# Hybrid encoder layer on one core: small operations of the attention stage issued some shares later, and the embedding's last product taken bank by bank

## The chip, the cores and the metric

One core of a Trainium2 chip runs the whole layer. The metric is the device time of one execution in microseconds; for the kernel before, the median of three runs is 1230.82 us.

## The reference

One post-norm encoder layer in float32 on 1024 tokens of width 1024:

```
u   = x @ W_in                                     # q,k,v,gate of 8 retention heads; q,k,v of 8/2 attention heads
R   = bidirectional chunkwise retention (chunks of 128), group norm, times silu(gate)
A   = windowed grouped attention (+-128 tokens), ALiBi, sink logit
h   = LN1(alpha*x + concat(R, A) @ W_out)
f   = (silu(h@W_gate) * (h@W_up)) @ W_down  +  sigmoid(h @ W_pg) * (p @ W_pe)
out = LN2(alpha*h + f)
```

The second term of f is the per-token embedding gate: W_pg is 1024 x 1024, p is 1024 x 256.

## The kernel before

Products of float32 matrices are made of three matmuls: each operand is split into a rounded part hi (an ACT copy) and a rest lo (a DVE subtraction), and `mm3` (L78) or `mm3c` (L847) multiplies hi*hi, hi*lo and lo*hi. `split` (L72) issues the two operations.

The program has these stages, in order of time:

- the first projections (to about 60 us);
- attention and retention, in "runs" (60 to 375 us): first Attention 0, then Retention 0, then three pairs of Retention i and Attention i;
- the output projection with LN1 (375 to 475 us);
- the embedding gate (to about 590 us), which is a one-level Strassen product: seven products `product(p, ...)` of 48 matmuls each into sets of four PSUM banks, then half tiles `embed(t, h, ...)`;
- gate/up of the feed-forward part and the down projection (to the end), Strassen again, in an order written out by hand.

In the attention stage only TensorE's order is written out (`manual_schedule` for PE); the other engines' order is made by the framework's planner, from its own estimate of times. The same planner orders all engines, PE too, in the embedding gate. `behind(ins)` (L83) adds no wait: it tells the planner to place an instruction after the latest `mm3`. A function `run(steps, total)` goes through a list in which each F (None) is a *share*: `total` projection steps (one `mm3` each) are spread evenly over the shares, and after each share one entry of the list `side` is executed. `side` carries the presplits: `presplit_small` splits p and W_pe, `presplit_gate` makes the seven Strassen operands of W_pg for four contraction tiles k, each with 7 splits and 4 DVE sums, and stores them to DRAM. Its entries are one load, one empty share and seven splits per k. Raw weights pass through `rawt`, two buffers of the tag raw.

Names in the attention stage: `Attention.scores(n)` multiplies (L499, L500), applies bias and maximum on DVE (L501), exponentiates on ACT (L505), takes the reciprocal of the sum (L507) and scales (L509); `turn(n)` transposes the scaled block (L517); `values(n)` multiplies with v (L529). `Retention.keys(q)` transposes keys (L378) and decays them (kdec, L381), `kv(q)` multiplies (L392) and masks (L396), `scores(hh)` makes pt (L420) and qq (L423), `out` accumulates, `norm(hh)` normalises: sums, squares, the power -0.5 on POOL (L463) and the product with it (L464). `turn(hh)` transposes and evicts to y (L471). The decay tables qd and dt are made in `Retention.__init__` (L362 to L370), with POOL's mask product and sum.

In the embedding gate, `stream` loads split operands through eight weight buffers (w and u). `product` has two forms: bank outermost (each bank finished before the next) and, with `outer=True`, contraction outermost. `embed(t, h, x, ...)` multiplies p's tile with W_pe (6 matmuls), takes sigmoid(x) on ACT (L905), multiplies (L906) and adds into the accumulator (L908), and stores the whole accumulator tile to the DRAM buffer zd (L910) after its second half. For the first four half tiles p comes through tag p, two buffers of 256 KB (L899); for the last twelve through tag ln, two buffers of 512 KB that hold two token tiles each (L889). The last product (p=3) carries eight half tiles, two behind each bank; four more follow it. `s1`, an operand of eight of them, lies in the two raw buffers. The first gate/up weights are loaded by `Pair.load` (L981) into raw and ln buffers, called in the preparation of the first units.

Of the kernel before, what the change touches and what calls it, by code (L numbers as in the profile page):

```python
# [16 lines left out]
P = 128  # L17
# [12 lines left out]
NSC = 4  # L30

# [9 lines left out]
def layer(tc, xT, xn, w_first, w_mt, w_rv, w_out, w_pg, w_pe, pT, w_gu, w_dn,  # L41
# [310 lines left out]

    class Retention:


        def __init__(self, i, y):
            self.i, self.y = i, y
            self.rk, self.rq, _ = pairs[i]
            self.A = [bt([P, NT - 1, P], f"kv{d}") for d in range(2)]
            self.kdec, self.pt, self.qq, self.ym = {}, {}, {}, {}  # L360
            self.qd = bt([P, 2, P], "qd")
            for d, c in ((0, C_QF), (1, C_QB)):  # L362
                act.activation(self.qd[:, d, :], cst[:, c:c + P], AF.Exp, scale=lg[:, 16 + 4 * d + i:17 + 4 * d + i])
            self.dt = bt([P, 2, P], "dt")
            for h in range(2):
                e = bt([P, 2, P], "sq", 1)
                act.activation(e[:, 0, :], cst[:, C_DP:C_DP + P], AF.Exp, scale=lg[:, 2 * i + h:2 * i + h + 1])
                act.activation(e[:, 1, :], cst[:, C_DN:C_DN + P], AF.Exp, scale=lg[:, 8 + 2 * i + h:9 + 2 * i + h])
                pool.tensor_tensor(e, e, masks, ALU.mult)
                pool.tensor_tensor(self.dt[:, h, :], e[:, 0, :], e[:, 1, :], ALU.add)  # L370
# [80 lines left out]
        def norm(self, hh):  # L451
            o = self.o
            og = o.rearrange("p n (h e) -> p (n h) e", h=2)
            sm = bt([P, 3, 8], "sm", 2)
            dve.tensor_reduce(sm[:, 0, :], og, AX.X, ALU.add, negate=True)
            ym = self.ym[hh] = bt([P, 8, 64], "ym", 2)
            dve.scalar_tensor_tensor(ym, sm[:, 0, :].unsqueeze(2).to_broadcast([P, 8, 64]), 1.0 / 64, og,
                                     ALU.mult, ALU.add)
            sq = bt([P, 8, 64], "sq", 1)
            act.activation(sq, ym, AF.Square)  # L460
            dve.tensor_reduce(sm[:, 1, :], sq, AX.X, ALU.add)
            dve.tensor_scalar(sm[:, 1, :], sm[:, 1, :], 1.0 / 64, EPS, ALU.mult, ALU.add)  # L462
            pool.tensor_tensor(sm[:, 2, :], sm[:, 1, :], cst[:, C_MH:C_MH + 1].to_broadcast([P, 8]), ALU.pow)  # L463
            dve.tensor_tensor(ym, ym, sm[:, 2, :].unsqueeze(2).to_broadcast([P, 8, 64]), ALU.mult)  # L464
# [12 lines left out]
    class Attention:  # L477
# [6 lines left out]
        def scores(self, n):  # L484
# [22 lines left out]
            dve.reciprocal(st_[:, 3, j, :], st_[:, 2, j, :])  # L507
            for g in range(2):
                act.activation(sc[g][:, :nk], sc[g][:, :nk], AF.Copy, scale=st_[:, 3, j, g:g + 1])  # L509
# [38 lines left out]
    def presplit_small():  # L548

        o = a_tile([P, 2, HF], "pro", "A0", F32R)  # L550
        hold = {}

        def load(n):
            r = hold[n] = rawt(2 * HF)
            if n < 2:
                for j in range(4):
                    sp.dma_start(r[:, j * 2 * P:(j + 1) * 2 * P], pT[4 * n + j])
# [6 lines left out]
        return [f for n in range(4) for f in (lambda n=n: load(n), None, lambda n=n: step(n, 0), None, None,  # L564
                                              lambda n=n: step(n, 1))]

    def presplit_gate():

        raw = [a_tile([P, 2, HF], "pre", "A1") for _ in range(2)]
# [3 lines left out]
        def load(k):  # L573
            for j in range(2):
                sp.dma_start(raw[j], w_pg[j, k])

        def steps(k):

# [10 lines left out]
            return [lambda: load(k), None, s(1, a11), s(4, a22), s(2, a12), s(5, a22, (a22, a21, a22, ALU.add)),  # L589
# [3 lines left out]
        return [f for k in range(4) for f in steps(k)]  # L593
# [35 lines left out]
    def run(steps, total):  # L629

        shares = steps.count(None)
        done = n = 0
        for f in steps:
            if f is None:
                n += 1
                take(total * n // shares - done)
                done = total * n // shares
                if side:
                    (side.pop(0) or (lambda: None))()
            else:  # L640
                f[0](*f[1:])

    F = None
    with tc.manual_schedule(engines={mybir.EngineType.PE}):
# [7 lines left out]
             F, trn(6), F, trn(7), F, val(6), val(7), F], 64)  # L652
        assert not side
        side.extend(presplit_gate())
        r = Retention(0, ytile(0))
# [4 lines left out]
             Y(0, 0), F, Y(0, 1), N(0), F, Q(1), F, F, Y(1, 0), F, Y(1, 1), N(1), F, F], 48)  # L660
        for i in range(1, NPAIR):
            if i == 2:
# [3 lines left out]
            a = Attention(i, ytile(2 * i + 1))  # L666
            run([K(0), Q(0), F, X0, F, C(0), F, X1, K(1), F, C(1), sco(0), F,
                K(2), F, C(2), sco(1), F, K(3), F, trn(0), sco(2), F, C(3), (r.scan,), F, trn(1), F,
                sco(3), F, val(0), val(1), F, trn(2), Y(0, 0), F, sco(4), F, Y(0, 1), N(0), trn(3), F, sco(5), F,
                val(2), val(3), Q(1), F, trn(4), F, F, sco(6), F, trn(5), F, Y(1, 0), F, sco(7), F, val(4), val(5), F,  # L670
                Y(1, 1), N(1), trn(6), F, trn(7), F, F, val(6), val(7)], 48)
# [212 lines left out]
    ptile = {}  # L884

    def load_p(j):

        ptile[j] = ct([P, 2, HF], "ln", 2, F32R)
        sp.dma_start(ptile[j].bitcast(F32), ptd[j])  # L889

    def embed(t, h, x, wpe, tag):

        if ptile:
            if t % 2 == 0:
                load_p(t // 2)
            pt = ptile[t // 2][:, :, (t % 2) * 2 * P:(t % 2 + 1) * 2 * P]
        else:
            pt = ct([P, 2, 2 * P], "p", 2, F32R)
            sp.dma_start(pt.bitcast(F32), ptd[t // 2][:, :, (t % 2) * 2 * P:(t % 2 + 1) * 2 * P])  # L899
# [9 lines left out]
        if h == (0 if t >= 4 else 1):  # L909
            sp.dma_start(zd[t], accs[t])  # L910

    def pair_of(f, g):
        def both():
            f()
            g()
        return both
# [15 lines left out]
    for k in range(4):  # L932
        embed(k, 0, X[k], wpe, "to"[k % 2])
    Z = four("b")
    product(5, Z, True, TT[1], steps[4:6])
# [8 lines left out]
    product(4, Y, False, TT[4])  # L944
    add4(s1, s1, Y)
    wpe = [stream(ped[1, q]) for q in range(2)]
    ptile[-1] = None
    both_ = [pair_of(lambda t=t, x=x: embed(t, 1, x[t % 4], wpe, "mm"), lambda t=t, x=x: embed(t + 1, 1, x[t % 4 + 1], wpe, "s"))
             for t, x in ((0, s1), (4, c22), (2, s1), (6, c22))]
    product(3, Z, False, HB[1, 1], both_)  # L950
    wpe0 = [stream(ped[0, q]) for q in range(2)]
# [546 lines left out]
```

## Time and profile before

| | us |
|---|---|
| median of three runs | 1230.82 (1227.77 to 1234.38) |
| the profiled execution | 1232.8 |
| its span, first to last instruction | 1231.0 |
| TensorE busy | 1202.4 (98%) |
| VectorE (DVE) busy | 732.0 (59%) |
| ScalarE (ACT) busy | 510.1 (41%) |
| GpSimd (POOL) busy | 366.7 (30%) |
| mean granted TensorE clock | 0.992 |

A row of the timeline has the start, the time, the engine, the line, the operation and its tiles; brackets give how long the engine sat idle before it and what ended that. SPq is the queue of SyncE, which issues the loads and stores in order. A row of waits has the waiting engine and line, what ended the wait, the total, the number and the longest. DVE and ACT run their instructions in order, so an instruction that waits holds up those behind it.

### The profile page before, as it was taken

How to read it: one execution, taken by the hardware profiler on the slowest of the kernel's cores; microseconds unless marked ns; L12 is line 12 of the kernel's file. 1: busy time of each engine (PE TensorE's matmuls, PEld its weight loads, DVE VectorE, ACT ScalarE, POOL GpSimd, SP SyncE). 2: the span in 40 equal slices, each digit the busy share in tenths (PEclk: the TensorE clock that was granted, in tenths of full speed). 3: DMA queues.
4: the chain of work that ended last, by engine and by line, in shares of the span. 5: the costliest groups of instructions: out<-in, count | busy, mean ns of one | idle time of the engine just before them, and what ended most of it. 6: DMA issues, size and time to landing. Idle time of an engine off the chain costs nothing.

```text
span 1231.0 us, 16420 instructions
## 1 busy us (share of the span) xinstructions
PE 1202.4 (98%) x5939; PEld 995.7 (81%) x5939; DVE 732.0 (59%) x1262; ACT 510.1 (41%) x960; POOL 366.7 (30%) x342
## 2 busy tenths in 40 slices
PE   9999989999999999999799999999999999999996
PEld 7878878888888888787688888888888888888885
DVE  4542688765646387946655544555445555875667
ACT  4565246655775114302333332332323334652463
POOL 2000021201110020000566656466565523034232
PEclk9999999999999999999899999999999999999999
DMA  6243446410103315467431133322233149999977
GB/s 244 69 139 130 150 164 224 170 35 18 35 18 122 101 52 208 143 247 239 155 128 70 69 118 128 129 78 77 103 129 129 69 145 279 383 277 212 258 181 205
DMA packets 67568, 179.48 MB, mean 146 GB/s; under 512 B 7968, under 2 KB 10144, under 8 KB 67488
## 3 DMA queue, kind: packets, MB, share of 16 engines
q1 hardware_dynamic: 58848, 161.66, 37.1%
q0 software_dynamic: 8640, 16.78, 7.7%
q8 instruction: 47, 0.77, 0.2%
q14 instruction: 33, 0.27, 0.1%
HBM read 125.72 MB, written 47.45 MB: 141 GB/s over the span
## 4 chain that ended last, share of the span: by engine, by line
PE 88%; DVE 4%; DMA 3%; ACT 2%; issue 1%; POOL 1%; SPq 0%; DVEq 0%; ACTq 0%; POOLq 0%
PE bmm L79 6%; PE bmm L80 5%; PE bmm L81 5%; PE bmm L849 5%; PE bmm L850 5%; PE bmm L851 5%; PE bs L849 5%; PE bs L851 5%; PE bs L850 5%; PE bo L851 4%; PE bo L850 4%; PE bo L849 4%; PE bt L849 4%; PE bt L851 4%; PE bt L850 4%; PE bo L529 1%
## 5 line engine op out<-in xcount | busy, mean ns | idle before, releaser
L79 PE MATMUL bmm<-H,w 128*128 128x512 f32 x240 | 100.6, 419 | 0.6 <-ACT H L73 0.6
L81 PE MATMUL bmm<-H,w 128*128 128x512 f32 x240 | 94.6, 394 | 0.0
L80 PE MATMUL bmm<-H,w 128*128 128x512 f32 x240 | 94.4, 393 | 0.0
L989 POOL TENSOR_TENSOR H<-ln 128x512 f32<-128x512 f32 x22 | 29.4, 1335 | 193.6 <-DMA ln<-in_w_gu 193.6
L1019 POOL TENSOR_TENSOR ev<-ev 128x512 f32<-128x512 f32 x33 | 55.7, 1687 | 92.4 <-DVE ev L1034 40.9
L74 DVE TENSOR_TENSOR w<-raw,w 128x512 fp32r<-128x512 f32 x64 | 50.5, 798 | 53.4 <-ACT w L73 53.2
L496 POOL COPY sc<-skb 128x1 f32<-128x1 f32 x64 | 16.7, 269 | 209.2 <-PE bt L517 187.0
L74 DVE TENSOR_TENSOR w<-H,w 128x512 fp32r<-128x512 f32 x44 | 39.6, 900 | 62.7 <-ACT w L73 62.7
L1017 ACT ACTIVATE ev<-ev 128x512 f32<-128x512 f32 x33 | 20.9, 633 | 104.8 <-DVE ev L1034 104.8
L1023 POOL TENSOR_TENSOR ev<-ev,ev 128x512 f32<-128x512 f32 x44 | 62.0, 1420 | 2.6
L74 DVE TENSOR_TENSOR u<-H,u 128x512 fp32r<-128x512 f32 x47 | 36.5, 777 | 38.7 <-ACT u L73 38.4
L501 DVE CUSTOM_DVE_ANT_0 sc<-cst,bs,skb 128x384 f32<-128x384 f32 (+1 forms) x64 | 35.3, 576 | 31.0 <-PE bs L500 30.9
L81 PEld LDWEIGHTS bmm<-H,w 128*128 128x128 f32 x240 | 45.3, 189 | 10.2
L79 PEld LDWEIGHTS bmm<-H,w 128*128 128x128 f32 x240 | 45.4, 189 | 9.8 <-ACT H L73 1.5
L73 ACT ACTIVATE w<-raw 128x512 fp32r<-128x512 f32 x64 | 39.3, 623 | 31.4 <-PE bmm L81 13.0
L80 PEld LDWEIGHTS bmm<-H,w 128*128 128x128 f32 x240 | 45.6, 190 | 6.3
L505 ACT ACTIVATE sc<-sc,st 128x385 f32<-128x385 f32 (+1 forms) x64 | 37.1, 582 | 27.2 <-DVE st L503 27.1
L73 ACT ACTIVATE u<-H 128x512 fp32r<-128x512 f32 x47 | 29.6, 631 | 39.7 <-PE bs L851 11.1
L721 POOL TENSOR_TENSOR stt<-stt,cst 128x1 f32<-128x1 f32 x8 | 11.6, 1454 | 97.9 <-DVE stt L720 97.9
L74 DVE TENSOR_TENSOR u<-raw,u 128x512 fp32r<-128x512 f32 x26 | 31.9, 1226 | 10.4 <-ACT u L73 10.4
L463 POOL TENSOR_TENSOR sm<-sm,cst 128x8 f32<-128x8 f32 x8 | 14.6, 1830 | 77.4 <-DVE sm L462 77.4
L993 POOL TENSOR_TENSOR H<-raw,H 128x512 f32<-128x512 f32 x22 | 37.4, 1698 | 0.0
(819 smaller groups left out, 3764.6 us busy)
## 6 DMA issues: line engine op xcount, KB each, us to landing
ad<-ev SPq DMA_DIRECT2D x33, 512.0 KB, 2.6
pgd<-pro SPq DMA_DIRECT2D x28, 512.0 KB, 2.9
raw<-in_w_gu SPq DMA_DIRECT2D x22, 512.0 KB, 4.3
ln<-in_w_gu SPq DMA_DIRECT2D x22, 512.0 KB, 3.5
raw<-ad SPq DMA_DIRECT2D x40, 256.0 KB, 5.6
ln<-ad SPq DMA_DIRECT2D x37, 256.0 KB, 6.5
H<-in_w_dn SPq DMA_DIRECT2D x33, 256.0 KB, 7.1
raw<-in_w_mt SPq DMA_DIRECT2D x14, 512.0 KB, 3.9
```

What stands on the lines that cost most here:

```text
L73: act.activation(hi, raw, AF.Copy)
L74: dve.tensor_tensor(lo, raw, hi.bitcast(F32), ALU.subtract)
L79: pe.matmul(o, lh, rh, start=start, stop=False)
L80: pe.matmul(o, lh, rl, start=False, stop=False)
L81: recent[0] = pe.matmul(o, ll, rh, start=False, stop=stop).ins.name
L505: act.activation(sc[g][:, :nk + 1], sc[g][:, :nk + 1], AF.Exp, bias=st_[:, 1, j, g:g + 1], accum_out=st_[:, 2, j, g:g + 1])
L849: pe.matmul(o, lh, rh, start=start, stop=False, skip_group_check=True)
L850: pe.matmul(o, lh, rl, start=False, stop=False, skip_group_check=True)
L851: pe.matmul(o, ll, rh, start=False, stop=stop, skip_group_check=True)
L993: pool.tensor_tensor(s[3], a(0, 1), s[0], ALU.subtract)
L1019: pool.tensor_tensor(c[:, 1, :], c[:, 0, :], c[:, 1, :], ALU.mult)
L1023: pool.tensor_tensor(self.ev[dst][:, 0, :], left, right, op)
```

## The change

Five things are changed together.

1. **Later issue in the attention stage.** `run` keeps a list `later`: an entry is executed a given number of shares after it was put there. The reciprocal and the two scalings of a softmax block go two shares later (LAG), the last product of a retention norm too. The decay tables of pair i+1 are made at the end of pair i (`decay_q`, `decay_k`), those of pair 0 at the end of Attention 0. All these are placed `behind` the latest `mm3`.
2. **presplit_small** begins four shares later and has one empty share less per load.
3. **presplit_gate**: tiles k=0 and k=1 are loaded ahead of Retention 0 (k=1 into two buffers of its own, tag A0) and split in its 14 shares without a pause; k=2 is loaded at share 8 and split from pair 1's share 2 on, every second share; k=3 follows.
4. **Embedding, products 5 and 4** have the contraction outermost.
5. **Embedding, the last product**: after each of its four banks, `last_tiles(k)` adds what completes a block and issues two, four, three and three half tiles. All p tiles come through tag p (two buffers of 256 KB, `load_p(t)`), every half tile stores its half of zd, W_pe's two halves are loaded together, and after the first and second bank the first gate/up loads are issued.

```diff
+    def decay_q(i):
+        qd = bt([P, 2, P], "qd")
+        decays[i] = qd, bt([P, 2, P], "dt")
+        for d, c in ((0, C_QF), (1, C_QB)):
+            behind(act.activation(qd[:, d, :], cst[:, c:c + P], AF.Exp, scale=...))
+    def decay_k(i, h):
+        e = bt([P, 2, P], "sq", 1)
+        behind(act.activation(e[:, 0, :], ..., AF.Exp, ...))
+        behind(act.activation(e[:, 1, :], ..., AF.Exp, ...))
+        pool.tensor_tensor(e, e, masks, ALU.mult)
+        pool.tensor_tensor(decays[i][1][:, h, :], e[:, 0, :], e[:, 1, :], ALU.add)
 ...
-            dve.tensor_tensor(ym, ym, sm[:, 2, :]..., ALU.mult)
+            later.append([2, lambda: behind(dve.tensor_tensor(ym, ym, sm[:, 2, :]..., ALU.mult))])
 ...
-            dve.reciprocal(st_[:, 3, j, :], st_[:, 2, j, :])
-            for g in range(2):
-                act.activation(sc[g][:, :nk], sc[g][:, :nk], AF.Copy, scale=st_[:, 3, j, g:g + 1])
+            def scaled():
+                behind(dve.reciprocal(st_[:, 3, j, :], st_[:, 2, j, :]))
+                for g in range(2):
+                    behind(act.activation(sc[g][:, :nk], sc[g][:, :nk], AF.Copy, scale=st_[:, 3, j, g:g + 1]))
+            later.append([LAG, scaled])
 ...
-        return [f for n in range(4) for f in (load(n), None, step(n, 0), None, None, step(n, 1))]
+        return [None] * 4 + [f for n in range(4) for f in (load(n), None, step(n, 0), None, step(n, 1))]
 ...
-        raw = [a_tile([P, 2, HF], "pre", "A1") for _ in range(2)]
+        first, other = ([a_tile([P, 2, HF], "pre", t) for _ in range(2)] for t in ("A1", "A0"))
 ...
-            return [lambda: load(k), None, s(1, a11), s(4, a22), s(2, a12), s(5, ...), s(7, ...), s(6, ...), s(3, ...)]
-        return [f for k in range(4) for f in steps(k)]
+            return [s(1, a11), s(4, a22), s(2, a12), s(5, ...), s(7, ...), s(6, ...), s(3, ...)]
+        load(0)
+        load(1)
+        k0, k1, k2, k3 = map(steps, range(4))
+        k1[0] = pair_of(k1[0], lambda: load(2))
+        return k0 + k1 + [None] + gap(k2, range(6)) + [lambda: load(3), None, None] + gap(k3, (1, 4))
 ...
                 if side:
                     (side.pop(0) or (lambda: None))()
+                for x in list(later):
+                    x[0] -= 1
+                    if not x[0]:
+                        later.remove(x)
+                        x[1]()
 ...  (in the runs: decay_q and decay_k of the next pair behind three of the last shares)
-    def embed(t, h, x, wpe, tag):
+    def embed(t, h, x, wpe, tag, pt):
 ...
-        if h == (0 if t >= 4 else 1):
-            sp.dma_start(zd[t], accs[t])
+        sp.dma_start(zd[t][:, sl], accs[t][:, sl])
 ...
-    product(5, Z, True, TT[1], steps[4:6])
+    product(5, Z, True, TT[1], steps[4:6], True)
 ...
-    product(4, Y, False, TT[4])
+    product(4, Y, False, TT[4], outer=True)
 ...
-    both_ = [pair_of(embed(t, 1, ...), embed(t + 1, 1, ...)) for t, x in ((0, s1), (4, c22), (2, s1), (6, c22))]
-    product(3, Z, False, HB[1, 1], both_)
-    for k in range(4):
-        dve.tensor_tensor(u2[k], u2[k], Z[k], ALU.add)
-        embed(4 + k, 0, u2[k], wpe0, ("s", "o", "s", "o")[k])
 ...
-            if p == 1:
+            if p == 1 and n:
                 pr.load(m)
 ...
+    def last_tiles(k):
+        dve.tensor_tensor(u2[k], u2[k], Z[k], ALU.add)
+        for t, h in ([(0, 1), (1, 1)], [(2, 1), (3, 1), (4, 1), (4, 0)], [(5, 1), (5, 0), (6, 1)], [(6, 0), (7, 1), (7, 0)])[k]:
+            if t not in pt:
+                pt[t] = load_p(t)
+            turn_[0] += 1
+            x = s1[t] if t < 4 else (u2 if h == 0 else c22)[t - 4]
+            embed(t, h, x, wpe[h], ("s", "mm")[turn_[0] % 2], pt[t])
+        if k < 2:
+            pairs2[0].load(k)
+    pt, turn_ = {}, [0]
+    w3 = [stream(pgd[2, kt]) for kt in range(4)]
+    wpe = [[stream(ped[h, q]) for q in range(2)] for h in (1, 0)][::-1]
+    for k in range(4):
+        c = slice(k * P, (k + 1) * P)
+        for kt in range(4):
+            mm3c(Z[k], HB[1, 1][:, 0, kt, c], HB[1, 1][:, 1, kt, c], w3[kt][:, 0, :], w3[kt][:, 1, :], False, kt == 3)
+        last_tiles(k)
```

More of the change, by code (lines that the diff above doesn't have):

```diff
@@ L30 @@
 NSC = 4
+LAG = 2
 C_ID, C_DP, C_DN = 0, 128, 256
@@ L360, in __init__ @@
             self.kdec, self.pt, self.qq, self.ym = {}, {}, {}, {}
[L361 to L370, printed above, removed]
+            self.qd, self.dt = decays[i]
         def keys(self, q):
@@ L574, in load @@
             for j in range(2):
-                sp.dma_start(raw[j], w_pg[j, k])
+                sp.dma_start((other if k == 1 else first)[j], w_pg[j, k])
         def steps(k):
+            raw = other if k == 1 else first
             (a11, a21), (a12, a22) = ([raw[j][:, i, :] for i in range(2)] for j in range(2))
@@ L587, in s, with pair_of, both @@
                 return f
-            return [lambda: load(k), None, s(1, a11), s(4, a22), s(2, a12), s(5, a22, (a22, a21, a22, ALU.add)),
+            return [s(1, a11), s(4, a22), s(2, a12), s(5, a22, (a22, a21, a22, ALU.add)),
                     s(7, a21, (a21, a11, a21, ALU.subtract)), s(6, a11, (a11, a22, a11, ALU.subtract)),
                     s(3, a12, (a12, a12, a11, ALU.subtract))]
-        return [f for k in range(4) for f in steps(k)]
+        load(0)
+        load(1)
+        k0, k1, k2, k3 = map(steps, range(4))
+        gap = lambda fs, at: [f for n, g in enumerate(fs) for f in ((g, None) if n in at else (g,))]
+        k1[0] = pair_of(k1[0], lambda: load(2))
+        return k0 + k1 + [None] + gap(k2, range(6)) + [lambda: load(3), None, None] + gap(k3, (1, 4))
+    def pair_of(f, g):
+        def both():
+            f()
+            g()
+        return both
     side = []
@@ L651, in layer @@
              sco(4), F, trn(3), F, sco(5), F, val(2), val(3), F, trn(4), F, sco(6), F, trn(5), F, sco(7), F, val(4), val(5),
-             F, trn(6), F, trn(7), F, val(6), val(7), F], 64)
-        assert not side
+             F, trn(6), (decay_q, 0), F, trn(7), (decay_k, 0, 0), F, val(6), val(7), (decay_k, 0, 1), F], 64)
+        assert not side and not later
+        y0 = ytile(0)
         side.extend(presplit_gate())
-        r = Retention(0, ytile(0))
+        r = Retention(0, y0)
         K, C, N = (lambda q: (r.keys, q)), (lambda q: (r.kv, q)), (lambda q: (r.norm, q))
```

47 lines of the change are left out of this document (19 added, 28 removed).

## The prediction

> **What bounds the kernel now.** I read the page first, then the waits of TensorE (PE), the granted clock in stretches, and the timeline around each long wait.
>
> ```profile
> PE 1202.4 (98%) x5939; PEld 995.7 (81%) x5939; DVE 732.0 (59%) x1262; ACT 510.1 (41%) x960; POOL 366.7 (30%) x342
> ...
> 600.00:1031.00 431.00, 431.00 (x1903) 356.98 (x1903) 229.00 (x287) 135.80 (x230) 243.39 (x167) 1.00 0.32 112
> ```
>
> PE is the bound: 1202.4 of 1231.0 us. The second row is a stretch (time, then busy time of PE, PEld, DVE, ACT, POOL, granted clock, DMA share): 1903 matmuls in 431 us are 0.2265 us each, with nothing to win. The change adds and removes no matmul, so it can only move PE's idle time and the stretches of low clock. The waits of PE (total, times, longest):
>
> ```profile
> PE bmm L849 <- ACT u L73: 7.6, 1, 7.6
> PE bt L392 <- DVE kdec L381: 2.4, 3, 1.3
> PE bmm L849 <- DMA w<-pgd: 2.3, 1, 2.3
> PE bt L378 <- ACT y L471: 1.6, 1, 1.6
> ...
> PE bmm L79 <- ACT qq L73: 0.9, 1, 0.9
> ...
> PE bt L378 <- DVE kv L396: 0.5, 1, 0.5
> ...
> PE bmm L80 <- DVE qq L74: 0.2, 1, 0.2
> PE bt L517 <- ACT sc L509: 0.2, 1, 0.2
> PE bt L849 <- DMA w<-pgd: 0.2, 1, 0.2
> ```
>
> Together 15.9 us. Three of these places also lower the clock (the column before DMA share):
>
> ```profile
> 173.50:183.75 10.25, 6.70 (x36) 4.88 (x34) 8.62 (x16) 4.23 (x9) 4.20 (x5) 1.00 0.34 118
> 183.75:187.20 3.45, 3.16 (x14) 3.06 (x15) 2.48 (x7) 0.63 (x1) 0.00 (x0) 0.54 0.64 256
> ...
> 504.30:508.00 3.70, 1.37 (x6) 1.02 (x6) 3.70 (x7) 1.67 (x3) 0.00 (x0) 1.00 0.99 342
> 508.00:511.45 3.45, 3.45 (x10) 2.65 (x10) 2.17 (x3) 1.64 (x2) 0.00 (x0) 0.54 0.23 90
> ...
> 590.00:596.80 6.80, 3.24 (x8) 2.55 (x9) 3.27 (x4) 2.67 (x5) 2.54 (x2) 0.51 0.29 110
> ```
>
> After each idle place PE runs a few us at half clock, which costs half of its busy time there: 1.6, 1.7 and 1.6 us.
>
> **The change part by part.** *1. First gate/up loads issued inside the embedding (largest term).*
>
> ```profile
> 580.40 6.20 SPq L910 DMA_DIRECT2D zd<-acc  x4
> ...
> 584.97 1.28 DVE L908 TENSOR_TENSOR acc<-acc,sg 128x512 f32<-128x512 f32 x1
> ...
> 586.69 0.38 SPq L981 DMA_DIRECT2D raw<-in_w_gu  x1
> ...
> 592.87 0.63 ACT L73 ACTIVATE u<-raw 128x512 fp32r<-128x512 f32 x1 [10.74 <-DMA raw<-in_w_gu]
> ...
> 593.56 0.80 PE L849 MATMUL bmm<-h0a,u 128*128 128x512 f32 x1 [7.61 <-ACT u L73]
> ```
>
> The SP queue holds four zd stores from 580.40; the last waits for the add that ends at 586.25, and the w_gu load stands behind it, lands, is split on ACT, and only then PE goes on. The change calls this load behind half tile (4,0), with two banks and six half tiles (13.6 us of PE work, below) still to come; from issue to split it took 6.2 us (586.69 to 592.87). So 7.6 of waiting and 1.6 of clock go. Late next is the split behind the last sigmoids: one ACT operation of 0.63 us. I leave 0.6: **-8.6**, bounds -9.2 and 0 (the planner may keep the load behind stores).
>
> *2. The last product bank by bank, with p tiles of 256 KB in a ring of two.* Before, these twelve half tiles took p from 512 KB ln tiles; now eight loads share tag p. What such a load costs shows at 503:
>
> ```profile
> 503.19 1.88 SPq L899 DMA_DIRECT2D p<-ptd  x2
> ...
> 507.83 0.39 PE L79 MATMUL bt<-w,p 128*128 128x512 f32 x1
> ...
> DMA to landing us min/median/max: 4.2/6.0/6.9
> ```
>
> (the last row is that of tile p). A p tile is reloaded only when the half tiles of the one two before are multiplied. PE's work: a bank's 12 matmuls 2.7 us, a half tile's 6 matmuls 1.36; all 48 + 72 are 27.2 us. In written order, with 0.3 for the issue and 4.2 for landing: p2 can be there at 4.1 + 4.5 = 8.6 when PE wants it at 8.1, a wait of 0.5; p4 follows (2,1), which ends at 10.0, so it lands at 14.5, while PE is done with (3,1) at 11.3: 3.2. p5, p6 and p7 come in time behind the next bank's 2.7 us. PE is ordered by the planner here, which fills waits by its own estimate: at 506.84 it put four matmuls (0.9 us) in such a place. That leaves 0.5 + 2.3 = 2.8. A gap of 2.3 us at 504.3 was followed by half clock, one at 176 to 184 too, so I add half of 1.7. **+3.6**; bounds 0 (bank k=2 moved ahead of (4,1)) and +10.8 (6.9 us per load: 3.2 at p2, 5.8 at p4, 1.8 at p6).
>
> The Trainium skill, TensorE: Matmul & The Clock Gate, Part 1, says the clock falls back to half after a whole idle window of about 3.4 us. The trace disagrees: 2.33 us idle at 504.5 were enough. By the page's rule this term would be 2.8 and the forecast 0.8 lower.
>
> *3. Stores zd by halves.* 16 in place of 8; at some 0.3 us each that is 2.6 us more on SP, hidden under the 80 us of PE work between 503 and 586. Each waits for its add with the loads behind it in the queue. Near 505 these are weights of product 6, wanted only after product 5's 48 matmuls (10.9 us): 0. Between p loads, where also the four moved w_gu loads share the DMA engines, the cost is inside the upper bound of part 2.
>
> *4. Products 5 and 4 with the contraction outermost.* Same matmuls. A bank then needs one weight tile per 2.7 us instead of four, but four free banks at once: the add that reads the fourth bank has 3 x 0.68 = 2.0 us instead of 8.2. The adds take 0.69 each: 0, bounds -0.2 (the last row of PE's waits) and +1. The 2.3 us wait at 504 stays in my sum: p2 and p3 of the first four half tiles are loaded as before. Its bounds are -4.0 (product 5 fills it) and 0.
>
> *5. Pair 1's start, 172 to 187 us.*
>
> ```profile
> 175.18 1.15 DVE L464 TENSOR_TENSOR ym<-ym,sm 128x512 f32<-128x512 f32 x1 [1.54 <-POOL sm L463]
> ...
> 177.08 0.42 DVE L381 TENSOR_TENSOR kdec<-bt,kd 128x256 f32<-128x256 f32 x1
> ...
> 180.96 0.68 DVE L584 TENSOR_TENSOR pre<-pre 128x512 f32<-128x512 f32 x1
> ...
> 182.96 0.69 DVE L545 TENSOR_TENSOR pro<-pre,pro 128x512 fp32r<-128x512 f32 x1
> 183.56 0.75 DVE L381 TENSOR_TENSOR kdec<-bt,kd 128x256 f32<-128x256 f32 x2
> ...
> 176.68 0.40 ACT L367 ACTIVATE sq<-cst,lg 128x128 f32<-128x128 f32 x1 [2.65 <-POOL dt L370]
> ...
> 180.75 0.63 ACT L544 ACTIVATE pro<-pre 128x512 fp32r<-128x512 f32 x1 [2.04 <-DVE pre L584]
> 181.28 0.67 ACT L471 ACTIVATE y<-bt,gn 128x512 f32<-128x512 f32 x1
> ...
> 177.51 0.67 POOL L369 TENSOR_TENSOR sq<-sq,masks 128x256 f32<-128x256 f32 x1 [0.87 <-ACT sq L368]
> ...
> 182.01 0.44 PE L378 MATMUL bt<-cst,rkq 128*128 128x128 f32 x2 [1.62 <-ACT y L471]
> ```
>
> PE's three waits (1.3, 1.6, 0.9) each have a moved operation ahead of them: the norm product, which holds DVE until POOL's pow is done; the presplit's ACT copy, which waits for its DVE sum while the eviction L471 stands behind it; the presplit's DVE work ahead of kdec. After the change the four sums and four splits of tile k=1 are done earlier, and the first six shares of pair 1 hold three plain splits; the tables are built before the pair begins. A pair's tables are six ACT operations of 0.4 and four POOL ones of 0.7 us, now behind the last shares of the pair before; POOL's pow for N(1) is still ahead of them, and if they come late, DVE's first product with them (Q(0)) is late, a dozen shares ahead of its use: 0. Two p_g loads get buffers of their own and pass the last splits of k=0 on SP: 0, the splits wait for ACT and DVE. But N(1) is pinned two shares later, where DVE is held at 175 already, so the first wait may stay. I take 1.6 + 0.9 of waiting and 1.0 of the 1.6 of clock: **-3.5**, bounds -5.4 and 0. The 0.5 at 250, where pair 2 starts in the same way without presplit, goes with norm product and tables: **-0.5**, bounds -0.5 and 0.
>
> The same work is now in Retention 0:
>
> ```profile
> 127.00:172.00 45.00, 45.00 (x269) 38.54 (x268) 32.95 (x68) 13.07 (x23) 2.03 (x1) 1.00 0.47 164
> 172.00:241.00 69.00, 65.06 (x429) 54.92 (x428) 56.50 (x138) 45.25 (x105) 12.87 (x22) 0.98 0.55 206
> ```
>
> Its 14 shares hold 14 splits and 8 sums instead of 10 and 4: 8 x 0.69 = 5.5 us more DVE, 38.5 of 45 (86%). Pair 1 waited at 56.5 of 69 (82%). So **+1.0**, bounds 0 and +4 (what pair 1 lost moves here).
>
> *6. presplit_small four shares later.*
>
> ```profile
> 39.97 1.75 SPq L557 DMA_DIRECT2D raw<-in_pT  x4
> 42.39 21.28 SPq L330 DMA_DIRECT2D raw<-in_w_rv  x5
> ...
> 67.45 0.33 SPq L330 DMA_DIRECT2D raw<-in_w_rv  x1
> ```
>
> pT takes one of the two raw buffers from 40 to 63, so six w_rv loads go one by one, until PE waits for qq (0.9 + 0.2) near 70. With both buffers they end well earlier: **-1.1**, bounds -1.1 and 0.
>
> *7. Softmax scaling two shares later.* Per block one reciprocal and two scalings, then PE's transposes.
>
> ```profile
> L509 ACT ACTIVATE sc<-sc,st x64: 491/602/621, 61.0 to 368.1; 128x384 f32<-128x384 f32 x48, 128x256 f32<-128x256 f32 x16
> ```
>
> Some 1.6 us from issue to end (2 x 0.6, the reciprocal and two crossings). Pair 1 has 28 shares in 69 us, 2.5 each; the transposes come two or more shares after the new place, for block 7 one share. The cover is 0.9 us at block 7 and 3.3 elsewhere: 0, bounds -1 and +16 (0.5 at each of 32 blocks).
>
> **Sum.** -8.6 + 3.6 - 3.5 - 0.5 + 1.0 - 1.1 = -9.1. The profiled execution took 1232.8 (span 1231.0), so it would be 1223.7; the median of the three runs, 1230.82, lies 2.0 lower, so I forecast **1221.7**.
>
> **Rivals.** *The p ring eats the gain.* Against it: the planner fills. For it: landings up to 6.9 us and SP stores between. With +10.8 in part 2: 1221.7 + 7.2 = 1228.9, no change.
>
> *Everything is covered.* Part 2 at 0 and the wait at 504 filled: 1221.7 - 3.6 - 4.0 = 1214.
>
> *Slower: late scaling becomes what the transposes wait for.* PE now waits 0.2 us for it in all. ACT is busy 45.25 of 69 us in pair 1, so a queue of one or two operations (0.6 each) uses up block 7's cover. It makes the kernel slower by 0.5% (6.2 us) when the 32 blocks lose 15.3 us, 0.48 each; at 0.7 each, 22.4 us: 1244.
>
> *The load is not moved by the planner.* Part 1 at 0: 1230, no change.
>
> **How the numbers follow.** 0.5% of 1230.8 is 6.2 us, about what a measurement of this kernel can tell from no change. Forecast 0.54, everything covered 0.14, p ring 0.18, load not moved 0.06, slower 0.08. Faster is the first two: 0.68; same 0.24; slower 0.08. The range takes in the p ring and most of the covered case, 1211 to 1231; the forecast's own is 1216 to 1226.
>
> **What the changed profile would show.** Right: w_gu loads issued before the last zd stores, no wait of PE over 2 us and no half clock near 585; single-file w_rv loads gone; no half clock near 184. Part 2 shows as PE waiting for p in the embedding. Wrong would be: PE waiting for L509's successors in many blocks, for kdec or pt in Retention 0, or a half-clock stretch inside the embedding.

## The result and the profile after

| | before | after |
|---|---|---|
| median, same chip (5 runs each) | 1230.82 us (1227.24 to 1234.38) | 1218.51 us (1217.70 to 1222.02) |
| profiled execution | 1232.8 us | 1219.53 us |
| span | 1231.0 us | 1217.8 us |
| mean granted clock | 0.992 | 0.996 |

The median is 12.3 us lower, where 9.1 lower and 1221.7 were forecast. The ratio of the mean times is 0.9911, 95% interval 0.9883 to 0.9938, which is 11.0 us. First the busy row of the page, then what TensorE (PE) waited for after the change (engine and line, what ended the wait, total, times, longest).

```profile
PE 1197.5 (98%) x5939; PEld 992.0 (81%) x5939; DVE 729.1 (60%) x1262; ACT 510.1 (42%) x960; POOL 365.5 (30%) x342
```

```profile
PE bmm L884 <- DMA w<-pgd: 2.4, 1, 2.4
PE bt L402 <- ACT y L482: 1.5, 1, 1.5
PE bo L145 <- POOL sq L142: 1.3, 1, 1.3
PE bmm L80 <- DMA p<-ptd: 1.1, 1, 1.1
PE bmm L884 <- ACT sg L931: 0.8, 1, 0.8
PE bt L388 <- ACT y L482: 0.8, 1, 0.8
...
PE bt L402 <- DVE kdec L391: 0.2, 1, 0.2
```

The same 5939 matmuls are busy for 4.9 us less, since fewer of them run at half clock (some 1.9 of it in the first microseconds, by chance; see the last section). The wait of 7.6 for the split of the gate's first weight is gone; 0.8 for a sigmoid stands in its place. The three waits at pair 1's start (1.3, 1.6, 0.9) are now 1.5, 0.8 and 0.2, and qq is no longer waited for near 70 us. The weight wait of the embedding (2.3 before) is still there, and one for p (1.1) is new.

PE runs the same number of matmuls in every kernel, so the start of the nth matmul shows where two kernels drift apart. This table is worked out from the traces: microseconds won over the profiled execution of before, stage by stage. The stages end, in the trace of before, at 59.9 us (first projections), 73.7, 172.4 (end of Retention 0), 196.0 (pair 1's start), 475.4, 599.8 (embedding, first gate products) and the end.

| kernel | first proj. | to 74 | Ret. 0 | pair 1's start | to 475 | embedding | rest | all |
|---|---|---|---|---|---|---|---|---|
| after | 1.9 | 1.7 | -0.7 | 2.7 | 0.6 | 7.7 | -0.7 | 13.2 |
| embed_only | -0.5 | -0.3 | 0 | 0 | -0.2 | 7.5 | -0.2 | 6.4 |
| attention_only | 2.2 | 1.7 | -0.3 | 2.7 | -0.3 | -0.2 | 0.8 | 6.5 |
| late_load | 2.0 | 1.7 | -0.3 | 2.7 | 0.9 | 7.0 | -3.9 | 10.1 |
| bank_outer | 2.7 | 1.7 | -0.3 | 2.7 | 0.7 | 7.4 | -0.1 | 14.8 |
| p_ring_only | 1.4 | 0.1 | 0 | 1.6 | -0.6 | 8.1 | 0.3 | 10.8 |
| halves_only | 1.8 | -0.2 | 0 | 1.6 | -0.6 | 4.3 | 0.6 | 7.6 |
| old_presplit | 1.9 | 1.7 | 0.2 | -1.9 | -0.9 | 7.7 | -0.2 | 8.5 |
| old_small | 2.1 | -0.4 | -0.3 | 2.7 | -0.3 | 7.9 | 0.1 | 11.8 |
| norm_now | 0.2 | 1.7 | -0.3 | -2.1 | -0.4 | 6.1 | -0.1 | 5.2 |
| old_tables | 2.4 | 1.2 | -0.6 | 2.7 | 0.6 | 7.7 | 1.0 | 15.0 |
| scale_now | 2.3 | 1.7 | -0.3 | 2.7 | 1.0 | 8.1 | 0.9 | 16.4 |
| both_orders | 2.0 | 1.7 | -0.3 | 2.7 | 0.3 | 13.7 | 0 | 20.0 |

Each row is one execution; what its columns say of chance is in the last section. The -3.9 at the end of late_load comes from a single wait of 3.0 us for an accumulator at 1190.8 us with half clock behind it; that execution was the slowest of its kernel's four, and no other trace has such a wait there.

### The profile page after: what moved, and what is told of

Read it like the earlier page. It is cut to its first block, busy times and chain, and to the rows that moved or that the text cites. A ratio compares the mean times of both kernels' runs of the same rounds, so it can differ in the third digit from the quotient of the medians.

```text
span 1217.8 us, 16479 instructions
## 1 busy us (share of the span) xinstructions
PE 1197.5 (98%) x5939; PEld 992.0 (81%) x5939; DVE 729.1 (60%) x1262; ACT 510.1 (42%) x960; POOL 365.5 (30%) x342
## 4 chain that ended last, share of the span: by engine, by line
PE 69%; DMA 4%; DVE 3%; issue 3%; POOL 1%; ACT 1%; DVEq 0%; POOLq 0%; SPq 0%; ACTq 0%
PE bs L884 5%; PE bs L886 5%; PE bmm L884 5%; PE bs L885 5%; PE bmm L886 4%; PE bmm L885 4%; PE bt L884 4%; PE bt L886 4%; PE bt L885 4%; PE bo L884 4%; PE bo L885 4%; PE bo L886 4%; PE bmm L80 3%; PE bmm L81 3%; PE bmm L82 3%
## 5 line engine op out<-in xcount | busy, mean ns | idle before, releaser
L82 PEld LDWEIGHTS bmm<-H,w 128*128 128x128 f32 x240 | 45.0, 188 | 10.1
L74 ACT ACTIVATE w<-H 128x512 fp32r<-128x512 f32 x44 | 27.4, 622 | 23.0 <-PE bs L886 8.3
L473 POOL TENSOR_TENSOR sm<-sm,cst 128x8 f32<-128x8 f32 x8 | 14.3, 1783 | 73.7 <-DVE sm L472 73.7
```

The source lines that it names most:

```text
L74: act.activation(hi, raw, AF.Copy)
L82: recent[0] = pe.matmul(o, ll, rh, start=False, stop=stop).ins.name
```

## The experiments

**The two halves of the change, one at a time.** embed_only is the kernel before with the new embedding; attention_only is the kernel before with all the rest.

> The kernel before with the embedding part of the change alone (products 5 and 4, last product with its half tiles, early gate/up loads); attention stage as before. Theory (the two halves are independent): 7.7 us less than before, 1223.1 us; PE's wait of 7.6 us at the start of gate/up gone, a wait of about 1.1 us for a p tile instead. Rival (the embedding gains only because the attention half moved it in time against the loads): under 4 us less, over 1226.8.

> The kernel before with the attention part alone (later scaling, norm products and tables, both presplits); embedding as before. Theory: 4.5 us less (1.7 near 70 us, 3.0 at pair 1's start, 0.5 at pair 2's start, 0.7 given back in Retention 0), 1226.3 us, and the 7.6 us wait still there. Rival (the 1.6 us that the changed profile won in its first 26 us come from the change too): 6 us or more less, and the hundredth matmul starts 1.6 us earlier than in the profile before.

Against 1228.91 of the kernel before on their chip, embed_only took 1223.08 us (ratio 0.9942, 0.9919 to 0.9965) and attention_only 1225.73 (0.9973, 0.9961 to 0.9985): 5.8 and 3.2 less. The two ratios together make 0.9915, against 0.9911 of the whole change, so the two parts hardly touch each other: in the table each wins its own columns. (The first column is chance; see the last section.) attention_only keeps the long wait of before:

```profile
PE bmm L884 <- ACT u L74: 7.0, 1, 7.0
```

**Is it the place of the call?** late_load is the changed kernel with the gate's first loads called in the preparation of the units again.

```diff
-            if p == 1 and n:
+            if p == 1:
                 pr.load(m)
 ...
-        if k < 2:
-            pairs2[0].load(k)
```

> The changed kernel with the first gate/up loads issued in the preparation of the first units again, as before; half stores and the rest kept. Theory (the place of the loads is the cause): PE waits 6 to 8 us at the start of gate/up with half clock behind it, 8 to 9 us over the changed kernel, 1227. Rival (half stores free the SP queue, the loads' place does not matter): within 2 us of the changed kernel, 1218 to 1221.

It took 1219.8 us (0.9926, 0.9905 to 0.9946), and the long wait did not come back: the place of the call, which the prediction had named, is not the cause. The queue of SyncE in late_load shows why (start, time, operation):

```profile
548.50 0.38 SPq L991 DMA_DIRECT2D raw<-in_w_gu  x1
548.94 0.42 SPq L991 DMA_DIRECT2D ln<-in_w_gu  x1
...
558.19 0.59 SPq L991 DMA_DIRECT2D ln<-in_w_gu  x1
```

The planner puts the loads where its own estimate of times has them: raw at 548.50 and 555.71, ln at 548.94 and 558.19. The raw loads are as early as in the changed kernel (549.18 and 556.39; ln there at 517.56), though they are called later. In the kernel before the same planner had put the first ln load here:

```profile
577.25 0.32 SPq L889 DMA_DIRECT2D ln<-ptd  x1
579.97 0.33 SPq L981 DMA_DIRECT2D ln<-in_w_gu  x1
```

So the new theory: it could go no earlier, since p tiles passed through both ln buffers until 577, and the second raw load, which PE waited for, stood behind it and behind four stores. Two kernels made from the kernel before take the two apart. p_ring_only sends every p tile through the two p buffers; halves_only stores zd by halves.

```diff
 p_ring_only:
-    ptile[-1] = None
 halves_only:
-        if h == (0 if t >= 4 else 1):
-            sp.dma_start(zd[t], accs[t])
+        sp.dma_start(zd[t][:, sl], accs[t][:, sl])
```

> The kernel before with one edit: every half tile of the embedding takes its p tile of 256 KB through the ring of two p buffers; none goes through the two ln buffers. Order of the products, whole stores zd and the place where the gate's loads are called stay as before. In the written order of the SP queue the first gate/up ln load then stands ahead of the p loads of the last half tiles, and no longer behind the last of them. Theory now held (in the kernel before, the p tiles held the ln buffers, so that the gate's first loads could go out only when the last p tiles were multiplied): the wait of 7.6 us and the half clock behind it go, 7 to 9 us; twelve more p loads through two buffers give 1 to 5 us back as waits for p; time 1222 to 1227, from 1230. Rival (the half stores or the new order of half tiles free the queue): the wait of PE for the split of raw stays at 6 us or more and the time is 1229 to 1234. At the start of pair 1 all theories expect the waits of the kernel before.

> The kernel before with one edit: zd is stored by halves of 256 KB, each behind its own add, in all 16 half tiles. Theory of the ln buffers: the wait of 7.6 us before the gate stays at 6 us or more, since the last four p tiles still hold the ln buffers; the stores between the last p load and the gate's raw load are smaller, 0 to 1.5 us less; time 1229 to 1231. Rival (the four whole stores behind the last adds are what held the load): the wait falls under 3 us and the time is 1222 to 1225.

p_ring_only took 1222.01 us (0.9945, 0.9926 to 0.9964). Its queue, and PE's waits for p:

```profile
548.40 0.33 SPq L980 DMA_DIRECT2D raw<-in_w_gu  x1
548.78 0.42 SPq L980 DMA_DIRECT2D ln<-in_w_gu  x1
...
566.04 0.34 SPq L980 DMA_DIRECT2D raw<-in_w_gu  x1
566.43 0.42 SPq L980 DMA_DIRECT2D ln<-in_w_gu  x1
```

```profile
PE bs L79 <- DMA p<-ptd: 1.2, 2, 0.9
...
PE bo L79 <- DMA p<-ptd: 0.3, 1, 0.3
```

With the ln buffers free, raw and ln go out at 548 and 566 though the order of half tiles and the whole stores are those of before. The wait of 7.6 is gone (the longest left in the embedding is 2.2, for weights), 1.5 is paid for p, and 8.1 us are won in the embedding, all that the whole new embedding wins there (7.5 and 7.7). One line is enough for it.

halves_only took 1225.45 us (0.9967, 0.9952 to 0.9982), a miss for the theory as it was put: the wait fell to 2.8, not to 6 or more, and 4.3 us were won.

```profile
PE bmm L849 <- ACT u L73: 2.8, 1, 2.8
```

```profile
578.20 0.39 SPq L980 DMA_DIRECT2D ln<-in_w_gu  x1
579.13 0.32 SPq L909 DMA_DIRECT2D zd<-acc  x1
579.54 0.38 SPq L980 DMA_DIRECT2D raw<-in_w_gu  x1
```

Between the ln load and the raw load there is now one half store instead of four whole ones: 1.3 us from ln to raw (578.20 to 579.54) where it was 6.7 (579.97 to 586.69). The two causes stand in a row: the ln buffer sets when the pair of loads may start, the stores what the second load loses after it. Either edit takes most of the wait. With the ln buffers free, the smaller stores find nothing left to win: the whole new embedding, which has both, wins no more than p_ring_only.

**Products 5 and 4.** bank_outer is the changed kernel with their contraction innermost again.

```diff
-    product(5, Z, True, TT[1], steps[4:6], True)
+    product(5, Z, True, TT[1], steps[4:6])
-    product(4, Y, False, TT[4], outer=True)
+    product(4, Y, False, TT[4])
```

> The changed kernel with products 5 and 4 bank outermost again. Theory (this part is worth nothing): within 1 us, 1218 to 1220, the wait of 2.4 us for w near 498 as it is. Rival (contraction outermost saves waits for weights): 1 us or more slower, with new waits for w in products 5, 4 or 3.

1218.2 us (0.991, 0.9895 to 0.9925), and the weight wait is 2.2 instead of 2.4: this part of the change is worth nothing.

**The parts of the attention stage, each put back in the changed kernel.** In old_presplit the presplit of the first block weight is as before (one raw buffer, each load ahead of its steps, no gaps); in old_small presplit_small starts four shares earlier with two empty shares per load.

```diff
 old_presplit:
-        load(0)
-        load(1)
-        k0, k1, k2, k3 = map(steps, range(4))
 ...
-        return k0 + k1 + [None] + gap(k2, range(6)) + [lambda: load(3), None, None] + gap(k3, (1, 4))
+        return [f for k in range(4) for f in steps(k)]
 old_small:
-        return [None] * 4 + [f for n in range(4) for f in (load(n), None, step(n, 0), None, step(n, 1))]
+        return [f for n in range(4) for f in (load(n), None, step(n, 0), None, None, step(n, 1))]
```

> The changed kernel with the presplit of the first block weight put back as before: one raw buffer, each load directly ahead of its four steps, four blocks of shares back to back. The prediction's own step: PE's wait behind the presplit's ACT copy (1.6 us) and before kdec (0.9 us) at pair 1's start come back with about 1 us of half clock near 184: 2.5 to 3.5 us lost between matmuls 891 and 1000, and 0.3 to 1 us won in Retention 0 (matmuls 622 to 891); time 1220 to 1222. Rival (the decay tables and the norm product, moved away from there, made the room): pair 1's start stays within 0.7 us of the changed kernel and the time is 1218 to 1219.

> The changed kernel with the presplit of the small weights put back as before: first load four shares earlier, two free shares between the halves of a step. The prediction's own step: pT takes a raw buffer from 40 to 63 us again, the w_rv loads go one by one, and PE waits for qq near 70: 1.1 to 1.7 us lost between matmuls 242 and 300; time 1219.5 to 1220.5. Rival (the decay tables, gone from ACT near 30 us, made the room): that gain stays and the time is 1218 to 1219. No theory held has a reason for the first projections (matmuls 8 to 100), where every kernel with the new attention part was 1.6 to 2.3 us ahead so far in the same order of instructions: here they should be where the changed kernel has them, if it is a matter of the order; if they are where the kernel before has them, it is chance of the execution.

old_presplit took 1222.25 us (0.994, 0.9924 to 0.9957). Its timeline at pair 1's start (start, time, engine; in brackets the idle time before and what ended it):

```profile
177.63 0.63 ACT L559 ACTIVATE pro<-pre 128x512 fp32r<-128x512 f32 x1 [2.59 <-DVE pre L599]
178.17 0.67 ACT L482 ACTIVATE y<-bt,gn 128x512 f32<-128x512 f32 x1
...
178.89 0.44 PE L388 MATMUL bt<-cst,rkq 128*128 128x128 f32 x2 [3.14 <-ACT y L482]
180.92 2.08 PE L402 MATMUL bt<-rv,kdec 128*128 128x128 f32 x8 [0.89 <-DVE kdec L391]
```

This is the prediction's step as it was put: ACT's copy waits for its DVE sum, the eviction y behind it is late, and PE stands for 3.1 us. Spreading the presplit is worth 4.6 us at pair 1's start (2.7 against -1.9), more than the 2.5 to 3.5 expected: the clock records of old_presplit have half clock from 180.20 to 187.03, twice as long as in the kernel before. In Retention 0 it costs 0.5 to 0.9 (-0.3 to -0.7 with the spread presplit, 0.2 without).

old_small took 1221.44 us (0.9937, 0.9922 to 0.9952) and loses 2.1 us between 60 and 74 (1.7 against -0.4). SyncE's queue in old_small, then in the changed kernel:

```profile
39.64 22.18 SPq L331 DMA_DIRECT2D raw<-in_w_rv  x5
...
65.81 0.33 SPq L331 DMA_DIRECT2D raw<-in_w_rv  x1
```

```profile
37.04 17.10 SPq L331 DMA_DIRECT2D raw<-in_w_rv  x6
```

The six w_rv loads have been issued at 54 instead of 66. In that stage PE waits 1.6 us in old_small, of which 0.7 and 0.2 are for qq, and 0.1 in the changed kernel.

norm_now issues the norm product in its share again, old_tables builds the decay tables in `Retention.__init__` again, scale_now scales the softmax block in its share again.

```diff
 norm_now:
-            later.append([2, lambda: behind(dve.tensor_tensor(ym, ym, sm[:, 2, :]..., ALU.mult))])
+            dve.tensor_tensor(ym, ym, sm[:, 2, :]..., ALU.mult)
 scale_now:
-            later.append([LAG, scaled])
+            dve.reciprocal(...); two act.activation(..., AF.Copy, scale=...)
 old_tables:
-            self.qd, self.dt = decays[i]
+            (the twelve lines of the kernel before; decay_q and decay_k out of the runs)
```

> The changed kernel with the norm product issued in its share again, not two shares later. The prediction's own step: the product holds DVE until POOL's pow is done in either order, so the first wait at pair 1's start stays at 1.3 to 1.6 us and nothing else moves: between -0.5 and +0.5 us in each of the pairs, time 1217.5 to 1219.5. Rival (the two shares are what keeps DVE free for kdec and kv at the starts of the pairs): 1 to 3 us lost there, time 1220 to 1222.

> The changed kernel with the decay tables built again where a pair is set up, not behind the last shares of the pair before. The prediction's own step: at pair 1's start six ACT operations of 0.4 us and four POOL ones of 0.7 us stand before the evictions again: 0.5 to 2 us lost between matmuls 891 and 1000, 0 to 0.5 us at the start of each of the next two pairs; time 1219 to 1221. Rival (the presplit alone held pair 1's start): within 0.5 us everywhere, time 1217.7 to 1219.

> The changed kernel with the softmax scaling issued in its share again, not two shares later. The prediction's own step: ACT and DVE have time either way, so nothing moves: -1 to +1 us between matmuls 891 and 2300, time 1217.5 to 1219.5, PE's waits for sc 0.5 us or less in all. Rival one (the late scaling is near the transposes and costs already): 1 to 3 us won, time 1215.5 to 1217.5. Rival two (the scaling ahead of the evictions held the pairs' starts, and moving it brought a part of the gain): 1 to 3 us lost, time 1219.5 to 1221.5.

old_tables took 1217.39 us (0.9899, 0.9871 to 0.9926) and scale_now 1217.87 (0.9898, 0.9872 to 0.9925): neither can be told from the changed kernel. Both edits are worth nothing, and the expectation for the tables was a miss. For the tables the timeline says why. Two of their ACT operations at pair 1's start, in old_tables and then in the changed kernel:

```profile
172.84 0.40 ACT L386 ACTIVATE sq<-cst,lg 128x128 f32<-128x128 f32 x1 [1.82 <-POOL dt L389]
```

```profile
172.82 0.40 ACT L364 ACTIVATE sq<-cst,lg 128x128 f32<-128x128 f32 x1 [1.82 <-POOL dt L367]
...
174.16 0.69 ACT L482 ACTIVATE y<-bt,gn 128x512 f32<-128x512 f32 x1
174.90 1.05 PE L402 MATMUL bt<-rv,kdec 128*128 128x128 f32 x6 [1.52 <-ACT y L482]
```

The tables are written at the end of the pair before, but the planner runs the last of them at the start of the pair in both kernels, at the same time. ACT stands 1.8 us for POOL's sum, and the eviction y that ends PE's first wait comes behind them. So the edit moved the call and not the work; what pair 1's start would win with the tables out of the way was not tried.

norm_now was the larger miss: 1225.87 us (0.9965, 0.995 to 0.998). Before and at pair 1's start in norm_now, and POOL's power with the product behind it in the changed kernel:

```profile
167.35 0.63 ACT L558 ACTIVATE pro<-pre 128x512 fp32r<-128x512 f32 x1 [3.32 <-DMA pgd<-pro]
...
174.76 2.01 POOL L473 TENSOR_TENSOR sm<-sm,cst 128x8 f32<-128x8 f32 x1 [17.13 <-DVE sm L472]
...
176.81 1.15 DVE L474 TENSOR_TENSOR ym<-ym,sm 128x512 f32<-128x512 f32 x1 [1.53 <-POOL sm L473]
...
179.43 0.76 DVE L391 TENSOR_TENSOR kdec<-bt,kd 128x256 f32<-128x256 f32 x2
...
180.00 1.60 PE L402 MATMUL bt<-rv,kdec 128*128 128x128 f32 x6 [5.28 <-DVE kdec L391]
```

```profile
169.27 2.01 POOL L473 TENSOR_TENSOR sm<-sm,cst 128x8 f32<-128x8 f32 x1 [12.99 <-DVE sm L472]
...
171.32 1.15 DVE L474 TENSOR_TENSOR ym<-ym,sm 128x512 f32<-128x512 f32 x1 [1.54 <-POOL sm L473]
```

In both DVE is held 1.5 us until the power is done. But the power starts at 174.76 instead of 169.27, and kdec stands behind the product: 5.28 us of waiting, 4.8 us at pair 1's start (2.7 against -2.1). PE itself is 1.4 us behind the changed kernel there, so the chain of the norm ran some 4 us later against PE. The kernel before has the old norm product too and waits only 1.3 there, so what the later product saves is a loss that other parts of the change would bring with it. The first row points at the spread presplit: in norm_now one of its copies holds ACT for 3.3 us until an earlier operand is stored, just ahead of the norm, and the norm's first sum (DVE L465) comes at 170.08 instead of 164.50. That is read from one trace and not tested; a kernel with the old presplit and the old norm product together would tell.

**A better version.** The traces left two waits in the embedding: the weights of product 5 (2.4, with half clock behind) and p (1.1). both_orders changes two orders in the changed kernel: the first four half tiles go behind the four banks of product 2, and the last product's half tiles are spread 2, 2, 4, 4.

```diff
-    product(2, X, False, HB[1, 0], steps[0:4])
-    for k in range(4):
-        embed(k, 0, X[k], wpe, "to"[k % 2], load_p(k))
+    product(2, X, False, HB[1, 0], [pair_of(steps[k], lambda k=k: embed(k, 0, X[k], wpe, "to"[k % 2], load_p(k)))
+                                    for k in range(4)])
 ...
-        ... ([(0, 1), (1, 1)], [(2, 1), (3, 1), (4, 1), (4, 0)], [(5, 1), (5, 0), (6, 1)], [(6, 0), (7, 1), (7, 0)])[k]:
+        ... ([(0, 1), (1, 1)], [(2, 1), (3, 1)], [(4, 1), (4, 0), (5, 1), (5, 0)], [(6, 1), (6, 0), (7, 1), (7, 0)])[k]:
```

> A version meant to be better than the changed kernel, with two more changes of order in the embedding: the half tiles (0,0) to (3,0) run behind the four banks of product 2 instead of behind product 2, and the last product's half tiles are spread 2, 2, 4, 4 over its banks instead of 2, 4, 3, 3, so that two p tiles are wanted per bank. Theory (what is left there is the weight wait of 2.4 us near 498 us with 1.7 us of half clock behind it, since four half tiles of 1.36 us are all that PE has while the weights of product 5 land, and one p wait of 1.1 us at 561): both go, 3.5 to 5.2 us less than the changed kernel, time 1213 to 1215.5. Rival (the w and u buffers, freed by product 2's last matmuls, set when the weights of product 5 land, whatever lies before): the weight wait moves to the end of product 2 and grows by the half tiles now spent earlier, up to 5 us; the time is 1217 to 1224.

It took 1212.76 us (1211.42 to 1213.64), a little less than the 1213 to 1215.5 expected; the ratio to the kernel before is 0.9857 (0.9831 to 0.9883). Its stretch from 495 to 510 against that of the changed kernel (time, busy time of PE, PEld, DVE, ACT, POOL, granted clock, DMA share, GB/s), both_orders first:

```profile
495.00:510.00 15.00, 15.00 (x67) 12.41 (x67) 14.94 (x17) 3.21 (x4) 0.00 (x0) 1.00 0.85 295
```

```profile
495.00:510.00 15.00, 12.61 (x49) 9.98 (x48) 12.90 (x16) 3.31 (x4) 0.00 (x0) 0.89 0.80 280
```

67 matmuls instead of 49 in the same time: the weight wait is gone, with the half clock behind it. The trace has no wait for p either, and 13.7 us instead of 7.7 are won in the embedding.

## Why the prediction was right, and where it was not

The sum was right in sign and within 3.2 us: 9.1 less forecast, 12.3 measured. Two of its steps had the wrong cause (1, and the tables and the norm product in 5), so that the sum came out so near is in part luck. Its steps:

- **1, the gate's first loads (-8.6).** Size right: 7.6 of waiting and the half clock at 590 are gone, and 0.8 for a sigmoid stands where 0.6 was left. The cause failed, so the right size was partly luck: "The change calls this load behind half tile (4,0)" does nothing (late_load). What the change did was to free the ln buffers from p (p_ring_only: the whole gain) and to shorten the stores in the queue (halves_only: a good half of it). The row of four stores ahead of the raw load had been read; the ln load ahead of them, at 579.97, and what held it, had not.
- **2, the p ring (+3.6).** The term that was mis-sized: 1.1 us of waiting at p4, as placed, none at p2, and no half clock behind it. The planner put half of the last product's next bank (6 matmuls, 1.4 us) ahead of (4,1), on the way to the lower bound. The p tiles landed in

```profile
DMA to landing us min/median/max: 3.0/4.0/6.9
```

  against 4.2/6.0/6.9 before. The embedding won 7.7 where steps 1 and 2 together had 5.0; this is most of what the forecast was too high by.
- **3 and 4 (0).** No store held a load that PE waited for; the outermost contraction is worth nothing (bank_outer), and the wait of 2.3 stayed, as put, with the half clock behind it (501.11 to 504.52). The prediction had named half clock inside the embedding as a sign of being wrong, but this one was there before.
- **5, pair 1's start (-3.5).** 2.7 in the profiled executions. The presplit carries it, as the step said (old_presplit), and the first wait stayed (1.5), as it thought possible, but by another path: PE waits for the eviction y, which stands on ACT behind the tables and POOL's power, and no longer for kdec behind the norm product. "The tables are built before the pair begins" failed: the last of them still run at its start, in the same place with the old call (old_tables). The step saw no use in the later norm product; norm_now shows that without it 4.8 us would have been lost. Retention 0's +1.0 came out as 0.3 to 0.7. The half clock of before at 184 that the step counted was partly chance, see below.
- **6, presplit_small (-1.1).** 1.7 won in that stage, 2.1 lost when put back.
- **7, softmax scaling (0).** 0 (scale_now), and 0.2 us of waiting for sc as before; the rival that ended slower did not happen.

## What to carry to other kernels

A long wait for a load has two ends to look at: what stands ahead of it in the queue, and which buffer the loads ahead of it still need. Where a planner orders the work, moving a call may move nothing: here neither the gate's loads nor the decay tables followed their calls, and freeing the buffer did what the call could not. So look in the trace for where the work went. A part that is worth nothing by itself can be what keeps another part cheap, so test parts of a change by taking each out of the whole as well as by adding each alone.

## What the runs showed of the hardware

**The first microseconds differ from execution to execution.** The first projections start at half pace, though the granted clock of the rows reads 1.00 there. Stretches of the kernel before, then of the changed one:

```profile
6.00:9.00 3.00, 3.00 (x8) 2.31 (x7) 1.73 (x3) 0.60 (x3) 0.00 (x0) 1.00 0.96 364
```

```profile
6.00:9.00 3.00, 3.00 (x14) 2.42 (x14) 1.94 (x4) 1.02 (x3) 0.00 (x0) 1.00 1.01 386
```

The clock records kept with a trace begin only with the first change to full clock, at 9.92 us in before and 6.18 in after, and the view counts time without a record as full. The order of the first hundred matmuls is the same in all 14 traces, and yet this change comes anywhere from 4.24 to 10.74 us; in p_ring_only and halves_only, whose attention stage is that of before, at 7.24 and 6.33. Half of the time between two such changes is what the first column of the table shows: (9.92 - 6.18) / 2 = 1.87, against 1.9 for after, and within 0.1 in every row but attention_only (2.8 against 2.2). So the first column, up to 2.7 us, is chance, and a profiled difference of that size between two kernels needs the runs beside it.

**Half clock after short waits.** The 14 traces have 20 idle gaps of PE of 2.0 us or more (2.03 to 7.61 us). After 19 of them a stretch at half clock follows, some 3.4 us long after most; the one of 2.22 us near 498 in old_tables has none. Gaps of 1.0 to 1.5 us have none. The waits of 1.3, 1.6 and 0.9 us at pair 1's start of before are followed by one in before and embed_only, and by none in p_ring_only and halves_only, with the same waits in the same order of work. The stretch of p_ring_only that answers to 183.75 to 187.20 of before (x14, clock 0.54):

```profile
182.20:185.65 3.45, 3.13 (x21) 2.81 (x22) 3.39 (x10) 0.69 (x2) 0.00 (x0) 1.00 0.58 234
```

The clock records show what decides it. In every trace their changes lie whole multiples of 3.413 us apart (in before 174.08 us of full clock, 51 times that, then 3.413 of half, then 320.85 of full, 94 times). Cut into windows of this length, from the first record to the last matmul, the 14 traces have 4909 windows at full clock. In 21 of them PE is idle for 1.95 us or more, and half clock follows each; in all others it is idle for 1.89 us or less, and half clock follows none. So what counts in these traces is the idle time within one window, not the length of one gap. In before 1.42 us of the wait of 1.6 and 0.85 of that of 0.9 fall into the window that ends at 184.00; in p_ring_only the two fall into two windows, and so do the parts of the gap of 2.22 in old_tables (1.75 in the fuller one).

Where the windows lie against the kernel is a matter of chance. p_ring_only and halves_only are 1.6 us better at pair 1's start for no other reason, so of the 2.7 that the change won there 1.6 is this chance. Shifting the windows over the waits of before brings 1.9 us or more into one window in 28% of the positions, over those of the changed kernel in none, and over those of old_presplit in all. By this count the changed kernel's waits can no longer bring on that half clock, and it saves 1.6 us only in the executions that had it; as an estimate, 0.28 x 1.6 = 0.4 us on average.

The Trainium skill, TensorE: Matmul & The Clock Gate, Part 1, describes a window of about 3.4 us that runs free of the kernel. The multiples of 3.413 us agree with it. The page also asks for a whole idle window before the clock falls; that 18 of the 21 windows were idle for only 1.95 to 3.02 us and were followed by half clock does not agree.
